# A list scheduler's rule for GpSimd: two-input work only beside VectorE work that leaves the shared port alone

## The chip, the cores and the metric

The kernel runs on one core of a Trainium2 chip. Five engines with queues of their own work on it: TensorE (PE in the profile) multiplies matrices into PSUM, VectorE (DVE), ScalarE (ACT) and GpSimd (POOL) work element by element, and SyncE (SP) issues the DMAs. The metric is device time of one execution in microseconds; the kernel before takes 1488.42 us, the median of three runs (1487.71 to 1492.01).

## The reference

Two layers run on 512 latent tokens (`x`) and 256 context tokens (`ctx`), 1024 channels each. In each layer an adaptive scale and shift, computed from `c`, gives `h`; one wide projection `h @ w_in` feeds three branches; the branches are gated, projected, mixed by sigmoid gates and projected out, and a layer norm closes the residual:

```python
h = x * (1.0 + scale[:, None, :]) + shift[:, None, :]
(a_q, a_k, a_v, a_g, g_q, g_k, g_v, g_af, g_ab, g_g,
 s_u, s_v, s_g, m_a, m_g, m_s) = jnp.split(h @ p['w_in'], pts, axis=-1)
...
y_attn = blocked_attention(ql, k_all, v_all) * jax.nn.silu(a_g)
...
y_gla = gla_finish(ol_f + flip(ol_b), p['gla_o_norm'], x.dtype) * jax.nn.silu(g_g)
y_sgu = sgu(s_u, s_v, p['sgu_ln_g'], p['sgu_ln_b'], p['sgu_w'], p['sgu_b']) * jax.nn.silu(s_g)
...
def merge(ya, yg, ys, ga, gg, gs):
    m = (jax.nn.sigmoid(ga) * (ya @ p['w_br_attn'])
         + jax.nn.sigmoid(gg) * (yg @ p['w_br_gla'])
         + jax.nn.sigmoid(gs) * (ys @ p['w_br_sgu']))
    return m @ p['w_out']

out = merge(y_attn, y_gla, y_sgu, m_a, m_g, m_s)
x_new = layer_norm(DEEPNORM_ALPHA * x + gate[:, None, :] * out, p['post_g'], p['post_b'])
```

The attention branch is grouped-query attention with normalised, rotated queries and keys over 768 keys. The second branch is bidirectional gated linear attention. The third, the gating MLP (`sgu`), normalises `s_v`, mixes positions inside chunks of 128 by a matrix and multiplies by `s_u`. Layer 1 computes outputs for the latent tokens alone.

## The kernel before

All matmuls run in a 32-bit format of TensorE with each operand split into a high and a low part: `split` lets ScalarE round a tile to `hi`, and an operation with two inputs subtracts, `lo = raw - hi`; `mm3` then issues three matmuls (high by high, high by low, low by high). So every 256 KB piece of a weight that a DMA brings (`raw`) costs one ScalarE copy and one subtraction, and the same holds for the activations (`hlh`, `hll` for the latent tokens' high and low parts, `hch`, `hcl` for the context's; `mlh`, `mll` for the merged branches). Weight pieces have three `raw` buffers and five each of `hi` and `lo`; the PSUM tags `p`, `pt` and `s` have two buffers each.

The stages of a layer, by the labels in the code: the modulation and the projections of attention (`P1`), the projections of the linear attention (`gproj`), projections whose results are kept in DRAM for later (`fill`), attention (`att`), the decays (`decay`), linear attention (`gla`, tiles `M`, `Ac`, `Af`), the gating of the branches (`ag`, `gg`; `kept` is a gate that is read back, `yat` and `oT` the branch outputs), the gating MLP (`sgu`: `sv` is normalised and multiplied by the two rows of `sgc`, mixed on TensorE into `pt`, evacuated into `ymix`, then multiplied by `kept` and by `sg`), the three branch projections (`brA`, `brG`, `brS`; `sig` and `sgS` are the gates, `mac` the sum) and the output projection (`out`; `rA` and `rB` hold the residual). The `sgc` rows take the buffer of `yat`, and so are loaded when `yat` has been split into `yh` and `yl`. In layer 1 the gate of the output is multiplied into the weight (`raw<-raw,gate`).

The program is not issued in the order of the code. Each operation is recorded by class `Sched` with its inputs, outputs and an assumed cost, and `order` then plays the whole program through: at each step it takes the engine that is free first and the ready operation of the smallest priority number, and so fixes each engine's queue. `issue` repeats this; after each pass the priorities move a share `MIX` of the way from the old start times to the latest starts that the pass allowed, and the pass with the shortest assumed length is issued.

Many operations are recorded with two possible engines: `tta` (issued in line 128) may run an operation with two inputs on VectorE or on GpSimd, `evac` a copy out of PSUM on ScalarE or VectorE. Whichever engine comes to the operation first takes it, with one exception, a test for GpSimd, which the change edits. `_port` tells the scheduler which operations use the port that VectorE and GpSimd share: on GpSimd all that read SBUF, on VectorE those with two wide SBUF inputs and some copies; `held` is the time up to which an engine holds it.

In the profile, all operations that one engine was fixed for stand under the recorder's line 419 and all that had a choice under line 128, so rows are told apart by their tiles.

Of the kernel before, what the change touches and what calls it, by code (L numbers as in the profile page):

```python
# [27 lines left out]
class Sched:  # L28
# [109 lines left out]
    def order(self, prio):  # L138
# [3 lines left out]
        ops = self.ops  # L142
# [22 lines left out]
        free = dict.fromkeys(engs, 0.0)  # L165
        ready = {e: [] for e in engs}
# [5 lines left out]
        held = {"DVE": 0.0, "POOL": 0.0}  # L172
        other = {"DVE": "POOL", "POOL": "DVE"}
        seq, when = [], [0.0] * n
        gone = [None] * n
        why, byat, lastop, relby = [None] * n, [None] * n, {}, {}
        costs = [0.0] * n
        hold = [[] for _ in range(n)]
        put = ()
        ends = [0.0] * n  # L180

        def freed(x, e):
# [34 lines left out]
        while done < n:  # L217
            best = None
            for e in engs:
                L, R = later[e], ready[e]  # L220
                while L and (L[0][0] <= free[e] or gone[L[0][1]]):
                    a, i = heapq.heappop(L)
# [4 lines left out]
                t = free[e] if R else (L[0][0] if L else None)  # L227
# [7 lines left out]
            t, e = best  # L235
            R, L = ready[e], later[e]
            while L and L[0][0] <= t:
                a, i = heapq.heappop(L)
                if not gone[i]:
                    heapq.heappush(R, (prio[i], i))  # L240
            i = None
# [4 lines left out]
            if e == "ACT" and len(R) > 1:  # L246
                c = min(R, key=lambda x: x[0] + (self.SWITCH if ops[x[1]][5] not in (None, cur) else 0))
                R.remove(c)
                heapq.heapify(R)
                i = c[1]  # L250
            elif e == "PE" and len(R) > 1:
                while recent and recent[0][0] < t - self.TICK:
                    dense -= recent.popleft()[1]
                if dense < self.WARM and ops[R[0][1]][8] < 0.5:
                    c = min(R, key=lambda x: x[0] + (1e6 if ops[x[1]][8] < 0.5 else 0))
                    R.remove(c)
                    heapq.heapify(R)
                    i = c[1]
                else:
                    i = heapq.heappop(R)[1]  # L260
            elif e in held and R and held[other[e]] > t + 1.0:

                w = held[other[e]] - t
                c = min(R, key=lambda x: x[0] + (self.HOLD * w if e in self.port[x[1]] else 0.0))
                R.remove(c)
                heapq.heapify(R)
                i = c[1]
            else:
                i = heapq.heappop(R)[1]
            if gone[i]:  # L270
                continue
            if e == "POOL" and isinstance(ops[i][4], dict) and len(ops[i][4]) > 1 and i not in put:

                back = max(0.0, free["DVE"] - t) + sum(ops[j][4]["DVE"] if isinstance(ops[j][4], dict) else ops[j][4] for p_, j in ready["DVE"] if not gone[j] and p_ < prio[i])
                if back + ops[i][4]["DVE"] < self.LEAVE * ops[i][4]["POOL"]:
                    heapq.heappush(later["POOL"], (t + max(back, 100.0) + ops[i][4]["DVE"], i))
                    continue
            k = can(i)
# [86 lines left out]
        for i in reversed(seq):  # L365
            e = gone[i]
# [9 lines left out]
        return seq, late, when, gone, costs, why  # L376

    SWITCH = 100.0
    HOLD, LEAVE = 1.0, 1.0
    ROUNDS, MIX, ADJ = 12, 0.35, ("PE",)  # L380
    SAME = {"DVE": 127.0, "ACT": 148.0, "POOL": 96.0}
    AHEAD = 3000.0
    TICK, COLS, WARM = 10240 / 3, 3060.0, 5500.0
# [1208 lines left out]
```

## Time and profile before

| | |
|---|---|
| median of three runs | 1488.42 us |
| lowest, highest | 1487.71, 1492.01 us |
| the profiled execution | 1490.06 us, span 1488.3 us |
| mean granted clock of TensorE | 0.975 of full speed |
| TensorE, VectorE, ScalarE, GpSimd busy | 95%, 70%, 45%, 29% of the span |

The span runs from the first to the last instruction; about 1.8 us of the profiled execution lie around it. A busy share is a mean over stages that are limited by different things, so what counts is which wait ends last in a stage. TensorE's clock has two levels, 2.4 and 1.2 GHz; the granted share of a stretch is 1.00 or 0.50 for these, or lies between where a stretch holds both. A duration of VectorE or GpSimd contains the time in which the instruction stood in the engine and waited for a port.

### The profile page before, as it was taken

Reading aid. Unit: us, or ns where it says so; the run is one execution under the profiler, and the core shown is the slowest. Engines: PE = TensorE matmul, PEld = TensorE weight load, DVE = VectorE, ACT = ScalarE, POOL = GpSimd, SP = SyncE. Lnnn points to the kernel's source line nnn. Section 1 sums busy time; section 2 is a strip of 40 time slices with the busy share of each in tenths; the row PEclk is TensorE's granted clock in tenths of the full one; section 3 lists DMA queues with packets and bytes.
Section 4 is the critical chain, followed back from the end, with each engine's and each line's share of the span. In section 5 each row is a group of like instructions: output and inputs, shape, how many; then the busy total and the mean of one; then the engine's idle time right before and its main releaser. Section 6 shows DMA issues by size and latency. Waiting matters only on the chain.

```text
span 1488.3 us, 27349 instructions
## 1 busy us (share of the span) xinstructions
PE 1409.4 (95%) x10724; PEld 1246.0 (84%) x10724; DVE 1039.7 (70%) x1996; ACT 672.9 (45%) x1286; POOL 435.9 (29%) x472
## 2 busy tenths in 40 slices
PE   8899999999986999999999999999999949999977
PEld 5798899888875888888889999988988738888877
DVE  8968887896878777432166675888797875443496
ACT  4466666844461223222231365667845632422321
POOL 1443230465864000100000043320367650000164
PEclk9999999999997999999999999999999969999989
DMA  9410012332272654321233232012343355334342
GB/s 327 142 37 9 22 30 77 105 91 93 69 244 65 191 158 139 91 68 54 68 104 102 100 91 63 16 29 77 116 136 93 88 183 156 102 94 102 98 142 93
DMA packets 115891, 151.23 MB, mean 102 GB/s; under 512 B 8601, under 2 KB 89905, under 8 KB 115761
## 3 DMA queue, kind: packets, MB, share of 16 engines
q1 hardware_dynamic: 115762, 149.49, 33.0%
q8 instruction: 84, 1.38, 0.4%
q14 instruction: 45, 0.37, 0.1%
HBM read 134.76 MB, written 14.69 MB: 100 GB/s over the span
## 4 chain that ended last, share of the span: by engine, by line
PE 79%; DVE 8%; ACT 4%; POOL 3%; DMA 3%; issue 2%; SPq 0%; POOLq 0%; ACTq 0%; DVEq 0%
PE p L419 64%; PE pt L419 9%; PE s L419 5%; PE s L119 2%; DVE sm L419 1%; ACT L419 1%; DVE lo L128 1%; DMA wada<-in_w_adaT_dram 1%; ACT ez L419 1%; DVE junk L419 1%; POOL ymix L128 1%; DVE wada L419 1%; DMA raw<-in_w_in_dram 1%; DVE PTs L419 1%; DMA sgc<-in_sgu_ln_g_dram 1%
## 5 line engine op out<-in xcount | busy, mean ns | idle before, releaser
L128 DVE TENSOR_TENSOR lo<-raw,hi 128x512 fp32r<-128x512 f32 (+1 forms) x265 | 202.8, 771 | 227.4 <-ACT hi L419 218.8
L419 ACT ACTIVATE hi<-raw 128x512 fp32r<-128x512 f32 (+1 forms) x296 | 186.2, 634 | 235.4 <-PE p L419 155.9
L419 PE MATMUL p<-hlh,hi 128*128 128x512 f32 x704 | 281.8, 401 | 8.6 <-ACT sg L419 6.6
L419 PE MATMUL p<-hlh,lo 128*128 128x512 f32 x704 | 281.0, 400 | 1.4 <-POOL lo L128 1.1
L419 PE MATMUL p<-hll,hi 128*128 128x512 f32 x704 | 280.1, 399 | 0.0
L419 PEld LDWEIGHTS p<-hlh,hi 128*128 128x128 f32 x704 | 133.1, 189 | 36.4 <-ACT sg L419 6.8
L419 PEld LDWEIGHTS p<-hlh,lo 128*128 128x128 f32 x704 | 133.2, 189 | 31.3 <-POOL lo L128 1.3
L419 PEld LDWEIGHTS p<-hll,hi 128*128 128x128 f32 x704 | 133.0, 189 | 26.9
L419 PE MATMUL p<-hch,hi 128*128 128x256 f32 x368 | 105.3, 286 | 8.9 <-ACT sg L419 7.9
L419 PE MATMUL p<-hch,lo 128*128 128x256 f32 x368 | 105.4, 287 | 0.0
L419 PE MATMUL p<-hcl,hi 128*128 128x256 f32 x368 | 105.0, 285 | 0.0
L419 PE MATMUL p<-lo,hlh 128*128 128x256 f32 (+1 forms) x352 | 101.0, 287 | 1.1 <-DVE lo L128 1.1
L419 PE MATMUL p<-hi,hlh 128*128 128x256 f32 (+1 forms) x352 | 101.3, 288 | 0.7 <-ACT keep L128 0.7
L419 PE MATMUL p<-hi,hll 128*128 128x256 f32 (+1 forms) x352 | 100.2, 285 | 0.0
L128 POOL TENSOR_TENSOR M<-cs 128x192 f32<-128x192 f32 (+1 forms) x144 | 82.0, 598 | 17.7 <-DVE cs L419 5.7
L419 ACT ACTIVATE sig<-p 128x512 f32<-128x512 f32 (+1 forms) x48 | 25.2, 526 | 131.3 <-PE p L419 131.0
L419 PEld LDWEIGHTS p<-hch,hi 128*128 128x128 f32 x368 | 70.6, 192 | 11.3 <-ACT sg L419 8.1
L128 POOL TENSOR_TENSOR raw<-raw,gate 128x512 f32<-128x512 f32 x10 | 16.8, 1682 | 201.0 <-DMA raw<-in_w_out_dram 200.9
L419 ACT ACTIVATE P<-s,sm 128x768 f32<-128x768 f32 (+1 forms) x80 | 65.3, 820 | 19.5 <-DVE sm L419 19.2
L419 DVE SCALAR_TENSOR_TENSOR wada<-wada,srow 128x512 f32<-128x512 f32 x96 | 69.7, 734 | 5.4 <-DMA wada<-in_w_adaT_dram 4.0
L419 PEld LDWEIGHTS p<-hcl,hi 128*128 128x128 f32 x368 | 70.4, 191 | 2.0
L419 DVE TENSOR_TENSOR PTs<-pt,PTs 128x512 fp32r<-128x512 f32 x104 | 69.5, 685 | 3.5 <-ACT PTs L419 1.9
(320 smaller groups left out, 3665.3 us busy)
## 6 DMA issues: line engine op xcount, KB each, us to landing
raw<-in_w_in_dram SPq DMA_DIRECT2D x204, 256.0 KB, 2.9
wada<-in_w_adaT_dram SPq DMA_DIRECT2D x80, 256.0 KB, 4.9
raw<-in_w_out_dram SPq DMA_DIRECT2D x32, 256.0 KB, 3.0
raw<-in_w_in_dram SPq DMA_DIRECT2D x16, 272.0 KB, 2.9
wada<-in_w_adaT_dram SPq DMA_DIRECT2D x8, 512.0 KB, 6.2
raw<-in_w_br_attn_dram SPq DMA_DIRECT2D x16, 256.0 KB, 3.3
raw<-in_w_br_gla_dram SPq DMA_DIRECT2D x16, 256.0 KB, 3.2
raw<-in_w_br_sgu_dram SPq DMA_DIRECT2D x16, 256.0 KB, 2.9
```

The costliest lines, as they stand in the source:

```text
L119: return self.record(eng.n, lambda: [getattr(eng.e, m)(*a, **k) for m, a, k in calls], outs, ins, cost, None, dens)
L128: fns[p.n] = lambda real=real, k=k: real(**k)
L419: return s.record(n, lambda: real(*a, **k), outs, ins, _cost(n, meth, outs, ins, k), _table(n, k), _dens(n, ins, k), _port(n, meth, outs, ...
```

## The change

The test for GpSimd reads differently. Before, GpSimd left a two-engine operation to VectorE if VectorE, with the rest of its current operation, its ready operations of smaller priority number and this one, would be done sooner than GpSimd alone. After, only that part of VectorE's pending work counts which does not use the shared port: GpSimd leaves the operation if that part is shorter than 0.8 of what GpSimd would take, and looks at it again later. Besides, the scheduler makes 16 passes where it made 12, and moves priorities by 0.6 of the way where it moved them by 0.35. Nothing that is computed changes; the line numbers of the recorder grow by 2 (L419 becomes L421).

```diff
-        put = ()
...
-            if e == "POOL" and isinstance(ops[i][4], dict) and len(ops[i][4]) > 1 and i not in put:
-
-                back = max(0.0, free["DVE"] - t) + sum(ops[j][4]["DVE"] if isinstance(ops[j][4], dict) else ops[j][4] for p_, j in ready["DVE"] if not gone[j] and p_ < prio[i])
-                if back + ops[i][4]["DVE"] < self.LEAVE * ops[i][4]["POOL"]:
+            if e == "POOL" and isinstance(ops[i][4], dict) and len(ops[i][4]) > 1:
+
+                dve = lambda j: ops[j][4]["DVE"] if isinstance(ops[j][4], dict) else ops[j][4]
+                mine = [(dve(j), "DVE" in self.port[j]) for p_, j in ready["DVE"] if not gone[j] and j != i and p_ < prio[i]]
+                apart = max(0.0, free["DVE"] - max(t, held["DVE"])) + sum(c for c, p_ in mine if not p_)
+                back = max(0.0, free["DVE"] - t) + sum(c for c, _ in mine)
+                if apart < self.LEAVE * ops[i][4]["POOL"]:
                     heapq.heappush(later["POOL"], (t + max(back, 100.0) + ops[i][4]["DVE"], i))
                     continue
...
-    HOLD, LEAVE = 1.0, 1.0
-    ROUNDS, MIX, ADJ = 12, 0.35, ("PE",)
+    HOLD, LEAVE = 1.0, 0.8
+    ROUNDS, MIX, ADJ = 16, 0.6, ("PE",)
```

The order of the instructions on each engine shows what this moves. GpSimd's queue has 477 instructions before and 228 after, VectorE's 1822 and 2078.

GpSimd in the last stage of layer 1, where the weights of the output projection (`raw`) are multiplied by the gate and the merged branches get their low parts (`mll`); before:

```order
L128 TENSOR_TENSOR ymix<-ymix,sg 128x512
L128 TENSOR_TENSOR raw<-raw,gate 128x512 x2
L128 TENSOR_TENSOR mll<-mac_2149,mlh 128x512
L128 TENSOR_TENSOR raw<-raw,gate 128x512
L128 TENSOR_TENSOR mll<-mac_2150,mlh 128x512
L128 TENSOR_TENSOR raw<-raw,gate 128x512
L128 TENSOR_TENSOR lo<-raw,hi 128x512
```

GpSimd after, from the last copies of layer 1's linear attention on:

```order
L421 COPY Af<-Ac 32x4x32 x4
L421 TENSOR_SCALAR sg<-sg 128x4
L421 TENSOR_TENSOR sg<-sg,mhalf 128x4
L421 TENSOR_SCALAR sf<-sf 128x1
L421 TENSOR_TENSOR sf<-sf,mhalf 128x1
L421 TENSOR_TENSOR rA<-rA,pg 128x416 x2
```

All of the gating MLP, the branches and the output weights has left this queue; what remains is fixed to GpSimd.

VectorE in layer 1's gating MLP; before:

```order
L128 TENSOR_TENSOR sv<-sv,sgc 128x512 x5
L419 TENSOR_TENSOR ymix<-pt,sgc 128x4x128
L419 SCALAR_TENSOR_TENSOR wada,gs<-wada,srow 128x512
L419 TENSOR_TENSOR ymix<-pt,sgc 128x4x128
L419 SCALAR_TENSOR_TENSOR wada,gs<-wada,srow 128x512
L419 TENSOR_TENSOR ymix<-pt,sgc 128x4x128 x2
L128 TENSOR_TENSOR ymix<-ymix,kept 128x512 x2
L128 TENSOR_TENSOR ymix<-ymix,sg 128x512 x3
```

VectorE there after (`wada` is a product for the adaptive gate that is summed on the way):

```order
L128 TENSOR_TENSOR sv<-sv,sgc 128x512 x7
L421 TENSOR_TENSOR ymix<-pt,sgc 128x4x128
L128 TENSOR_TENSOR sv<-sv,sgc 128x512
L421 TENSOR_TENSOR ymix<-pt,sgc 128x4x128
L421 SCALAR_TENSOR_TENSOR wada,gs<-wada,srow 128x512
L421 TENSOR_TENSOR ymix<-pt,sgc 128x4x128
L421 SCALAR_TENSOR_TENSOR wada,gs<-wada,srow 128x512
L421 TENSOR_TENSOR ymix<-pt,sgc 128x4x128
L128 TENSOR_TENSOR ymix<-ymix,kept 128x512 x2
L128 TENSOR_TENSOR ymix<-ymix,sg 128x512 x2
```

All eight products of `sv` stand in this queue now, where three were on GpSimd, and the first two `sg` products follow two `kept` products at once.

TensorE just ahead of the same stage; before:

```order
L419 MATMUL p<-hll,hi 128x512
L419 MATMUL p<-hlh,lo 128x512
L419 MATMUL pt<-ident,o 128x128 x4
L419 MATMUL pt<-sgc,sv 128x128 x16
L419 MATMUL p<-hlh,hi 128x512
```

TensorE there after:

```order
L421 MATMUL p<-hlh,hi 128x512
L421 MATMUL p<-hll,hi 128x512
L421 MATMUL p<-hlh,lo 128x512
L421 MATMUL pt<-sgc,sv 128x128 x16
L421 MATMUL p<-hlh,hi 128x512
```

The mixing matmuls (`pt<-sgc,sv`) stood right behind the last transposes of the linear attention (`pt<-ident,o`); now projections stand between them. Between the last `s<-M` matmul of the linear attention and the first mixing matmul there are 18 matmuls of 512 columns before and 69 after in layer 1; in layer 0 there are 58 of 512 and 51 of 256 before, 71 and 67 after, and 24 of 256 and 2 of 512 after stand between the mixing matmuls.

## Rows read from the trace of the kernel before

**Rows 1.** The page's first part: busy time, share of the span and number of instructions of an engine.

```profile
span 1488.3 us, 27349 instructions
PE 1409.4 (95%) x10724; PEld 1246.0 (84%) x10724; DVE 1039.7 (70%) x1996; ACT 672.9 (45%) x1286; POOL 435.9 (29%) x472
```

**Rows 2.** The waits of TensorE over the whole span: who waited for whom, us in total, how often, the longest in us.

```profile
PE p L419 <- ACT sg L419: 14.5, 2, 7.9
PE pt L419 <- DVE sv L128: 13.5, 1, 13.5
PE s L419 <- ACT hlh L419: 8.5, 5, 2.4
PE pt L419 <- POOL sv L128: 8.4, 1, 8.4
PE p L419 <- DVE rA L419: 3.6, 2, 3.3
...
PE p L419 <- POOL mll L128: 1.9, 1, 1.9
...
PE p L419 <- ACT mlh L419: 1.4, 2, 0.7
...
PE p L419 <- DVE sgS L419: 0.8, 1, 0.8
```

**Rows 3.** Busy time by stretch, around the two gating MLPs: the stretch, its length, then busy us (and instructions) of PE, PEld, DVE, ACT and POOL, the granted clock of TensorE, the DMA share and GB/s.

```profile
452.00:458.00 6.00, 6.00 (x28) 6.00 (x29) 3.47 (x6) 0.00 (x0) 4.51 (x3) 0.50 0.00 0
...
469.20:475.20 6.00, 5.91 (x26) 5.81 (x27) 4.12 (x9) 1.02 (x3) 1.30 (x1) 0.50 0.03 12
...
1210.40:1216.00 5.60, 5.56 (x26) 5.57 (x27) 4.77 (x9) 0.00 (x0) 1.11 (x1) 0.51 0.24 80
...
1223.40:1229.50 6.10, 6.04 (x14) 4.78 (x15) 3.49 (x9) 3.15 (x5) 0.00 (x0) 0.50 0.18 37
```

**Rows 4.** Groups of VectorE's instructions from 1225 to 1400 us, a stretch in which GpSimd does nothing: line, engine, operation, tiles, shapes, count, then busy us, mean ns of one, idle us before them and what ended it.

```profile
L128 DVE TENSOR_TENSOR lo<-raw,hi 128x512 fp32r<-128x512 f32 x63 | 43.5, 691 | 89.0 <-ACT hi L419 88.9
...
L419 DVE TENSOR_TENSOR sig<-p,sig 128x512 f32<-128x512 f32 x8 | 5.5, 692 | 4.8 <-PE p L419 4.8
```

**Rows 5.** The same groups of VectorE from 1405 to 1441 us, the last stage, in which GpSimd works too (`sgS` reads `p` in PSUM).

```profile
L128 DVE TENSOR_TENSOR mac<-mac,sgS 128x512 f32<-128x512 f32 x7 | 10.2, 1464 | 0.0
L128 DVE TENSOR_TENSOR lo<-raw,hi 128x512 fp32r<-128x512 f32 x6 | 6.3, 1052 | 0.0
L419 DVE TENSOR_TENSOR sgS<-p,sgS 128x512 f32<-128x512 f32 x7 | 4.8, 680 | 0.6 <-PE p L419 0.6
```

**Rows 6.** GpSimd's largest group in the same stretch.

```profile
L128 POOL TENSOR_TENSOR raw<-raw,gate 128x512 f32<-128x512 f32 x8 | 14.1, 1769 | 186.3 <-DMA raw<-in_w_out_dram 186.2
```

**Rows 7.** VectorE's timeline at 1187 us: start, length of the merged piece in us, engine, line, operation, tiles, shapes, count.

```profile
1187.62 1.28 DVE L128 TENSOR_TENSOR lo<-raw,hi 128x512 fp32r<-128x512 f32 x2
```

**Rows 8.** The chain of work that ended last, pieces in order of time (start us, us, what), in the gating MLPs of layer 0 and layer 1.

```profile
442.45 4.30 DMA sgc<-in_sgu_ln_g_dram
...
450.23 1.71 POOL sv L128
...
451.99 5.50 PE pt L419 x24
...
462.77 6.06 POOL ymix L128 x3
...
1202.69 3.64 DMA sgc<-in_sgu_ln_g_dram
...
1208.64 1.76 DVE sv L128
...
1210.44 6.45 PE pt L419 x32
...
1217.68 5.11 POOL ymix L128 x3
...
1223.46 2.93 PE p L419 x6
```

**Rows 9.** Busy time by stretch as in rows 3, in the start, in layer 1's attention, in its linear attention and in its branch projections.

```profile
37.00:74.00 37.00, 32.59 (x167) 27.43 (x166) 36.61 (x97) 17.07 (x33) 17.18 (x13) 0.91 0.47 143
...
910.00:1050.00 140.00, 136.78 (x984) 126.31 (x983) 116.41 (x220) 92.23 (x197) 34.11 (x31) 1.00 0.14 39
...
1080.00:1120.00 40.00, 40.00 (x403) 32.49 (x402) 37.92 (x89) 19.76 (x41) 26.86 (x48) 1.00 0.45 126
...
1225.00:1355.00 130.00, 130.00 (x555) 105.18 (x554) 59.88 (x105) 43.10 (x73) 0.00 (x0) 0.98 0.40 112
```

**Rows 10.** Busy time by stretch of the instructions of line 128 alone, those that had a choice of engine: the stretch, its length, busy us (and instructions) of DVE, ACT and POOL, the granted clock, the DMA share and GB/s.

```profile
910.00:1050.00 140.00, 41.49 (x59) 3.15 (x7) 26.41 (x20) 1.00 0.14 39
...
1080.00:1195.00 115.00, 60.86 (x91) 6.74 (x12) 60.42 (x90) 1.00 0.40 115
...
1405.00:1445.00 40.00, 33.14 (x23) 0.00 (x0) 27.14 (x15) 0.87 0.40 132
```

**Rows 11.** The longest wait of VectorE over the whole span, columns as in rows 2.

```profile
DVE lo L128 <- ACT hi L419: 218.8, 87, 13.8
```

## The prediction

> **What bounds the kernel now.** I read the page's first part first. TensorE is busy 95% of a span of 1488.3 us, VectorE 70%, GpSimd 29% [rows 1]. So the most that a new division of work between VectorE and GpSimd can return is the time that TensorE stands still, and what its clock loses behind that. The waits of TensorE come next [rows 2]: the shown groups are 52.6 us, and four single waits make up most of it. 13.5 us and 8.4 us are for the first normalised tile of the gating MLP (`sv`), one in each layer, and 14.5 us in two waits (7.9, and 6.6 by difference) for ScalarE's `sg`, which itself waits for a buffer that a `ymix` product frees. Another 7.7 us are in the last projection (3.6 for `rA`, 1.9 for `mll` on GpSimd, 1.4 and 0.8). The start has 8.5 us.
>
> The two mixing stages show a second cost behind the waits, TensorE's clock [rows 3]: after the idle time it runs at its lower level of 1.2 GHz (granted 0.50 or 0.51) for 6.0 and 5.9 us of work in layer 0, 5.6 and 6.0 us in layer 1. Half of that is lost: 3 us each.
>
> Why the stages wait is read from durations. In a stretch where GpSimd has nothing to do a 128x512 subtraction of two SBUF tiles takes VectorE 691 ns, and one that reads PSUM 692 ns [rows 4]. In the last stage, beside GpSimd, the product `mac` takes 1464 ns and `lo` 1052 ns, while `sgS`, which reads PSUM, takes 680 ns [rows 5]. GpSimd needs 1769 ns for a product of that size there [rows 6]. Two VectorE subtractions back to back end in 1.28 us, so one costs its queue 0.64 us [rows 7].
>
> Here the Trainium skill, SBUF — State Buffer, Who interferes with whom, has a rule: a VectorE instruction with two SBUF inputs and a GpSimd instruction that reads SBUF exclude each other, and the later one blocks until the other ends. The trace agrees on who suffers (`mac`, not `sgS`) but not fully on how much: by a full block the 27.14 us of GpSimd in the last stage would all be lost to VectorE, while its 23 products there took 33.14 us [rows 10] for about 19.2 (by the order 16 of 0.64 and 7 of twice the width at 1.28), 13.9 lost. By the rule the last stage would give its whole 7.7 us of waits back; I go by the row, below.
>
> **The change part by part.** The new test leaves GpSimd a two-input operation only if VectorE has work without the port for at least 0.8 of its time. By the order, 248 of GpSimd's 327 such operations go to VectorE (30 of 31 `lo`, 84 of 144 `M<-cs`, all 10 `raw` products, 7 of 9 `sv`). All engines' queues are reordered by the new iteration; TensorE's instructions and the DMAs are the same set.
>
> *Layer 1's mixing.* Now the first `sv` products run from 1206.3, when `sgc` has landed, to 1210.4, and the `ymix` products on GpSimd take 5.11 us [rows 8]. TensorE restarts its large matmuls at 1223.46. After the change all eight `sv` are on VectorE: the first pair takes 2 x 0.64 = 1.3 us instead of 4.0. And the order puts 69 matmuls of 512 columns between the end of the linear attention and this point, 18 before. At 130 us for 555 [rows 9] one is 0.234 us, so 51 more are 11.9 us of cover. 11.9 + 2.7 is over 13.5: the first wait goes. Behind it the order has 15 VectorE operations up to the first `sg` product (6 `sv`, 4 `ymix<-pt`, 2 of the modulation, 2 `kept`, 1 `sg`), 9.6 us, where 12.4 pass now (1210.4 to 1222.8, the end of `ymix`): 2.8 saved. What is late next there is this VectorE queue alone, so some 4 us of the second wait stay, and its clock loss; the first clock loss (2.8) goes. Sum 13.5 + 2.8 + 2.8 = 19.1 us.
>
> *Layer 0's mixing.* The same way [rows 8]: `sgc` lands at 446.75 and TensorE starts at 451.99, 5.2 us that become 1.3 (3.9 saved). The cover is 13 matmuls of 512 and 16 of 256 columns more, 3.0 + 1.9 = 4.9 us. Together 8.8: the wait of 8.4 goes. Inside the stage the order now has 24 matmuls of 256 columns, 2.8 us, which weren't there. The VectorE queue to the first `sg` product is 18 x 0.64 + 2 x 0.96 (768 wide), 13.4 us, and one tile's two products stay on GpSimd, 2.6 us at twice VectorE's price: 16.0 against 16.9 (451.9 to 468.8). So 0.9 + 2.8 = 3.7 of the second wait, and 3.0 of clock. Sum 15.1 us.
>
> *The last stage.* 38 two-SBUF operations are now spread over 33.14 us of VectorE and 27.14 us of GpSimd in 40 us [rows 10]. All on VectorE they cost 30 x 0.64 + 8 x 1.28 = 29.4 us, and the PSUM reads among them (7 `sgS` at 0.68, some `rA` and statistics) about 7: 36.4, so 3.6 us less. Bounds 0 and the 7.7 of the waits; I take 4.
>
> *The start* (8.5 us of waits for `hlh` [rows 2]): VectorE is full there, 36.61 of 37 us [rows 9]. The 13 operations that keep GpSimd busy 17.18 us in that stretch come on top of it, at some 0.64 each 8 us, and the time that they take from VectorE by contention goes. I take +2, bounds -3 and +6.
>
> *What it costs.* The 51 and 13 matmuls were cover inside the linear attention. There the order has 66 fewer of 512 columns in layer 1 (15.4 us) and 33 of 512 with 16 of 256 fewer in layer 0 (9.6 us). Unless that stage becomes shorter by as much, TensorE waits in it instead. Its bound is the pair of engines: in 1080:1195 two-input work keeps VectorE busy 60.86 and GpSimd 60.42 us, together 121 in 115 [rows 10]. GpSimd's 90 operations there become 32. The 58 cost 58 x 0.67 = 38.9 us on GpSimd; on VectorE 42 small ones of 128 columns (an estimate: 0.3, half of what a four times wider one costs) and 16 at 0.64 are 22.8. That frees 16 us in layer 1, about the 15.4 that it must. Both ends: 0 and 25.0. Since a stage is not its busiest engine alone, I take 12, between the row and the worst end. Attention has VectorE at 116.41 of 140 us [rows 9] with 20 two-input operations on GpSimd, of which most move; their own contention goes with them too. Bounds -2 and +10, taken 3.
>
> Sum: 19.1 + 15.1 + 4 + 2 - 12 - 3 = 25 us off the profiled execution's 1490.06 (span 1488.3 and 1.8 around it): 1465. The runs' median, 1488.42, is 1.6 lower, so the forecast is 1463.5.
>
> **The rivals.** *The cover was only moved.* The linear attention does not get shorter, and the mixing is held by what VectorE never set (the `sgc` transfer of 3.64 and 4.30 us, ScalarE's `yh`). Then 25 us of new waits stand against half of the 34.2 and the 6 of the other two terms: 1490.1 - 23.1 + 25 = 1492, 1490.4 at the median. For it speaks that TensorE is already busy nearly everywhere and the total of its work is the same. Against it speak the two full port engines [rows 10].
>
> *VectorE becomes the bound.* Its queue is in order, and 248 operations more stand in it. Now `lo` waits for ScalarE's `hi` 87 times, 218.8 us, 2.5 each [rows 11]; while it waited, GpSimd took others. The 30 moved `lo` alone bring 75 us of such waits, and behind each stand the PSUM evacuations that free TensorE's banks. It decides where VectorE's row is full already, 37.92 of 40 us in 1080:1120 and 36.61 of 37 in 37:74 [rows 9]. If a quarter of the 75 falls there, 19 us, and the linear attention costs its full 25, the sum is 40.2 - 25 - 19 - 3 = -7: 1495 at the median, slower. Against it: contention there takes about as much of VectorE as the moved work needs. The Trainium skill, Perfetto Trace Analysis, Optimizing Scalar/DVE Operations, speaks for this rival: it says that with VectorE saturated handing work to GpSimd may make sense, though it adds that the shared port may undo it. By that rule the full rows above forbid the move; the trace's 1464 ns [rows 5] against 691 [rows 4] sides with its second half.
>
> *Nothing new waits.* Both costs are 0, the last stage gives 7.7 and the start 6: 19.1 + 15.1 + 7.7 + 6 = 48 us, 1440.5. Against it: so full a recovery needs each queue's new order to fit the chip's times.
>
> That the change does not do what it says is excluded by the order's counts.
>
> **How the numbers follow.** Forecast 0.62, cover only moved 0.12, VectorE the bound 0.10, nothing new waits 0.16. A measurement of this kernel can tell about 0.3%, 4.5 us, from no change. Forecast and last rival are faster, with a quarter of the first rival: 0.81. Of the first rival 0.07 more and of the second 0.02 are the same, 0.09; the rest, 0.10, is slower. The forecast's own range, with costs from 30 down to 2, is 1478 to 1450; to hold 8 of 10 beside the rivals on both sides it becomes 1447 to 1487.
>
> **What would show it.** Right: GpSimd's busy time falls from 436 us to about 140, VectorE's stays near 1040 (its products at 0.69 us again); the waits of 13.5 and 8.4 for `sv` are gone or under 2 us; GpSimd's name is gone from the chain in the mixing stages; `mac` in the last stage is under 0.8 us. Wrong: the waits of TensorE add up to 50 us or more as now, with new entries in the linear attention (`M`, `Ac`, `Af`), or in attention for `PTs` and `sm`, or VectorE's busy time rises above 1100 us.

## The result and the profile after

The changed kernel takes 1451.32 us (median of 4 runs, 1449.73 to 1453.14), the kernel before beside it 1488.74 us (4 runs). The ratio is 0.9745 with a 95% interval of 0.9724 to 0.9767: 37.4 us faster. The forecast was 1463.5 us, so the direction was right, the time lies inside the range, and the gain was half as large again as the 25 us forecast.

The first part of the page, after; it answers to [rows 1]:

```profile
span 1448.0 us, 27281 instructions
PE 1397.2 (96%) x10724; PEld 1232.3 (85%) x10724; DVE 1041.7 (72%) x2252; ACT 664.4 (46%) x1275; POOL 140.8 (10%) x223
```

GpSimd has lost two thirds of its work, and VectorE's busy time has grown by only 2.0 us although 248 operations came to it, since those that it already had became shorter: its 254 `lo` of 128x512 were busy for 192.3 us at 762 ns each, the 279 after for 191.6 at 693. The span is 40.3 us shorter. It splits into two parts: span less busy time of TensorE falls from 78.9 to 50.8 us, 28.1 us less standstill; and the same 10,724 matmuls are busy for 12.2 us less, at a higher granted clock (mean 0.994, before 0.975).

The waits of TensorE, after, in the columns of [rows 2]:

```profile
PE pt L421 <- DVE sv L128: 5.1, 2, 4.2
PE s L119 <- DVE M L128: 5.0, 5, 1.7
PE p L421 <- ACT sg L421: 3.9, 1, 3.9
PE s L119 <- DVE Ac L421: 3.0, 4, 1.3
...
PE s L421 <- ACT hlh L421: 2.3, 1, 2.3
```

The waits for `sv` fall from 21.9 us to 5.1 (0.9 in layer 0, 4.2 in layer 1), those for `sg` from 14.5 to 3.9. `Ac` is new and `M` has grown from 1.6 us to 5.0, both in the linear attention. All waits of TensorE add up to 41.0 us, before to 70.3.

Where the time went is read from stretches bounded by the same instructions in both kernels. Busy time by stretch, in the columns of [rows 3], before: the start up to the first scores; layer 0's linear attention (first to last matmul of `M`); layer 0's mixing (from there to 200 matmuls behind the last `pt<-sgc,sv`); layer 1's linear attention; layer 1's mixing (to 100 matmuls behind); the last stage (from its first output matmul to 300 before the end).

```profile
0.00:99.26 99.26, 88.45 (x474) 73.86 (x474) 82.57 (x220) 47.38 (x92) 29.61 (x33) 0.95 0.53 179
307.54:418.96 111.42, 110.08 (x1913) 95.71 (x1913) 92.89 (x168) 51.57 (x91) 78.41 (x105) 1.00 0.26 77
418.96:505.94 86.98, 68.95 (x402) 61.24 (x393) 64.83 (x107) 30.16 (x49) 34.64 (x24) 0.88 0.54 178
1092.16:1188.83 96.67, 96.08 (x1304) 76.69 (x1303) 83.00 (x174) 54.66 (x97) 66.41 (x104) 1.00 0.36 102
1188.83:1249.24 60.41, 39.23 (x201) 32.56 (x179) 40.77 (x65) 20.59 (x33) 19.00 (x13) 0.77 0.58 189
1421.68:1444.13 22.45, 15.41 (x85) 14.08 (x86) 22.28 (x19) 2.53 (x4) 17.11 (x9) 0.78 0.34 123
```

The same six stretches, after:

```profile
0.00:93.55 93.55, 84.14 (x468) 69.00 (x468) 76.26 (x233) 47.55 (x94) 6.24 (x16) 1.00 0.55 189
297.43:404.44 107.01, 101.92 (x1865) 88.06 (x1864) 97.45 (x216) 48.67 (x86) 38.37 (x58) 1.00 0.27 82
404.44:477.83 73.39, 72.44 (x457) 63.77 (x446) 55.73 (x109) 31.33 (x51) 4.49 (x4) 1.00 0.62 191
1069.52:1160.80 91.28, 82.49 (x1238) 65.53 (x1237) 82.03 (x211) 44.31 (x83) 27.34 (x51) 0.98 0.31 88
1160.80:1217.89 57.09, 49.05 (x251) 40.15 (x229) 39.91 (x76) 22.81 (x39) 1.20 (x2) 0.94 0.68 214
1389.49:1402.63 13.14, 10.72 (x86) 10.12 (x85) 13.14 (x18) 2.21 (x4) 0.00 (x0) 0.99 0.44 151
```

Since matmuls have moved between the stretches, a stretch is credited with what it now holds more and charged with what it holds less, each at the spacing that its kind had before. Layer 0's mixing is 13.6 us shorter and holds 9.6 us more: a gain of 23.2. The part of a gain that is standstill is the change of length less PE's busy time. The rest is the time that the matmuls themselves took more or less; where the granted clock rose with it, it is put down to the clock.

| stretch | forecast | gain | of it standstill | rest |
|---|---|---|---|---|
| start | 2 | 5.0 | 10.8 to 9.4: 1.4 | 3.6 |
| linear attention, layers 0 and 1 | -12 | -5.1, -9.9 | 1.3 to 5.1, 0.6 to 8.8: -12.0 | -3.0 |
| layer 0's mixing | 15.1 | 23.2 | 18.0 to 1.0: 17.1 | 6.1 |
| layer 1's mixing | 19.1 | 15.2 | 21.2 to 8.0: 13.1 | 2.1 |
| last stage | 4 | 9.3 | 7.0 to 2.4: 4.6 | 4.7 |
| attention, both | -3 | 0.4 | | |

The rows add up to 38.1 us of the 40.3 by which the span is shorter; the other 2.2 lie between these stretches.

Groups of VectorE in the last stage, after (1368 to 1401 us); they answer to [rows 5]:

```profile
L128 DVE TENSOR_TENSOR lo<-raw,hi 128x512 fp32r<-128x512 f32 x9 | 6.2, 686 | 1.8 <-ACT hi L421 1.8
...
L421 DVE TENSOR_TENSOR sgS<-p,sgS 128x512 f32<-128x512 f32 x8 | 5.5, 685 | 1.5 <-PE p L421 1.5
L128 DVE TENSOR_TENSOR mac<-mac,sgS 128x512 f32<-128x512 f32 x8 | 5.5, 684 | 0.0
```

`mac` has gone from 1464 ns to 684, `lo` from 1052 to 686, and `sgS`, which reads PSUM, has stayed (680, 685).

### The profile page after: what moved, and what is told of

It is laid out like the page before. It is cut to its first block, busy times and chain, and to the rows that moved or that the text cites. A ratio compares the mean times of both kernels' runs of the same rounds, so it can differ in the third digit from the quotient of the medians.

```text
span 1448.0 us, 27281 instructions
## 1 busy us (share of the span) xinstructions
PE 1397.2 (96%) x10724; PEld 1232.3 (85%) x10724; DVE 1041.7 (72%) x2252; ACT 664.4 (46%) x1275; POOL 140.8 (10%) x223
## 5 line engine op out<-in xcount | busy, mean ns | idle before, releaser
L421 PE MATMUL p<-hlh,hi 128*128 128x512 f32 x704 | 281.6, 400 | 6.1 <-ACT sg L421 3.9
L421 ACT ACTIVATE hi<-raw 128x512 fp32r<-128x512 f32 (+1 forms) x296 | 185.2, 633 | 220.0 <-PE p L421 145.4
L421 PE MATMUL p<-hll,hi 128*128 128x512 f32 x704 | 280.8, 399 | 0.0
L421 PE MATMUL p<-hlh,lo 128*128 128x512 f32 x704 | 280.5, 399 | 0.0
L421 PEld LDWEIGHTS p<-hlh,hi 128*128 128x128 f32 x704 | 132.7, 188 | 34.0 <-ACT sg L421 4.1
L421 PEld LDWEIGHTS p<-hlh,lo 128*128 128x128 f32 x704 | 132.9, 189 | 30.1 <-DVE lo L128 1.1
L421 PEld LDWEIGHTS p<-hll,hi 128*128 128x128 f32 x704 | 132.6, 188 | 26.2
L421 PE MATMUL p<-hch,lo 128*128 128x256 f32 x368 | 104.3, 283 | 0.0
L421 PE MATMUL p<-hcl,hi 128*128 128x256 f32 x368 | 104.3, 283 | 0.0
L421 PE MATMUL p<-hch,hi 128*128 128x256 f32 x368 | 104.2, 283 | 0.0
L421 PE MATMUL p<-hi,hlh 128*128 128x256 f32 (+1 forms) x352 | 101.7, 289 | 0.0
L421 PE MATMUL p<-hi,hll 128*128 128x256 f32 (+1 forms) x352 | 100.5, 286 | 0.0
L421 PE MATMUL p<-lo,hlh 128*128 128x256 f32 (+1 forms) x352 | 99.9, 284 | 0.0
L421 ACT ACTIVATE sig<-p 128x512 f32<-128x512 f32 (+1 forms) x48 | 25.3, 527 | 129.7 <-PE p L421 128.8
L421 POOL TENSOR_SCALAR sf<-sf 128x1 f32<-128x1 f32 x20 | 10.1, 505 | 687.5 <-DVE sf L421 687.0
L421 ACT ACTIVATE P<-s,sm 128x768 f32<-128x768 f32 (+1 forms) x80 | 65.3, 820 | 23.5 <-DVE sm L421 22.9
L421 DVE TENSOR_REDUCE sm<-s 128x1 f32<-128x768 f32 (+1 forms) x72 | 64.8, 921 | 9.6 <-PE s L421 9.5
L421 DVE TENSOR_TENSOR PTs<-pt,PTs 128x512 fp32r<-128x512 f32 x104 | 69.5, 684 | 2.7 <-ACT PTs L421 2.0
L421 PEld LDWEIGHTS p<-hch,hi 128*128 128x128 f32 x368 | 69.5, 189 | 2.0
L421 DVE SCALAR_TENSOR_TENSOR wada<-wada,srow 128x512 f32<-128x512 f32 x96 | 65.5, 689 | 7.7 <-DMA wada<-in_w_adaT_dram 6.3
L421 PEld LDWEIGHTS p<-hcl,hi 128*128 128x128 f32 x368 | 69.3, 188 | 2.1
```

Of the source, the lines that this page charges most:

```text
L421: return s.record(n, lambda: real(*a, **k), outs, ins, _cost(n, meth, outs, ins, k), _table(n, k), _dens(n, ins, k), _port(n, meth, outs, ...
```

## The experiments

Two causes had to be told apart: the freed port (which engine runs an operation) and the new order of all queues; and two parts of the change, the test and the larger steps. A third possible cause, that VectorE is simply the faster engine for such an operation (0.64 us for a product [rows 7], where GpSimd's shortest of that size takes 1.28), stands beside the port in the first pair of runs and is taken up at the added loads. "Kept" is the number of two-engine operations that GpSimd keeps; the kernel before has 327, the changed kernel 79. Matmuls and length of the linear attention are for layer 0 and layer 1, between the ends used above; each ratio is to the kernel before, run beside it.

| kernel | kept | us | ratio, 95% interval | linear attention, us | matmuls in it |
|---|---|---|---|---|---|
| before | 327 | 1488.7 | | 111.4, 96.7 | 1912, 1302 |
| changed | 79 | 1451.3 | 0.9724 to 0.9767 | 107.0, 91.3 | 1863, 1236 |
| old order, new engines | 79 | 1483.4 | 0.9945 to 0.9974 | 115.1, 98.2 | 1912, 1302 |
| new order, old engines | 327 | 1498.7 | 1.0048 to 1.0078 | 111.9, 88.8 | 1863, 1236 |
| test alone | 86 | 1446.1 | 0.969 to 0.9722 | 104.4, 93.0 | 1863, 1251 |
| steps alone | 325 | 1488.5 | 0.9989 to 1.0008 | 109.0, 97.6 | 1907, 1306 |
| none kept, large steps | 0 | 1475.3 | 0.9887 to 0.9923 | 116.7, 101.3 | 1936, 1295 |
| none kept, small steps | 0 | 1472.7 | 0.9873 to 0.9909 | 117.5, 98.6 | 1935, 1295 |
| test outside linear attention | 193 | 1462.7 | 0.9808 to 0.9839 | 111.1, 96.8 | 1917, 1288 |
| test in linear attention only | 223 | 1483.3 | 0.9947 to 0.9975 | 113.5, 96.2 | 1898, 1286 |
| share 0.5 | 111 | 1448.6 | 0.9703 to 0.9762 | 106.1, 89.1 | 1845, 1247 |
| share 1.2 | 41 | 1464.6 | 0.9817 to 0.9852 | 112.8, 95.4 | 1873, 1267 |

**Order and engines, one at a time.** The scheduler plans under both tests; the order of one plan is issued, and operations that may run on GpSimd take the engine of the other plan:

```diff
+        mine, other = self.plan(False), self.plan(True)
...
-            (fn[self.gone[i]] if isinstance(fn, dict) else fn)()
+            e = self.gone[i]
+            if isinstance(fn, dict) and "POOL" in fn:
+                e = other[3][i]
+            (fn[e] if isinstance(fn, dict) else fn)()
```

> The sequence of the kernel before, instruction by instruction, but every two-engine operation with GpSimd as a choice goes to the engine that the kernel after gives it (79 instead of 327 on GpSimd). Port theory (the gain comes from operations that no longer shut each other out): much of the 37 us is there without any new order, 1460 to 1475 us; mac in the last stage near 0.7 us, the last stage 5 us or more shorter. Order theory (the gain comes from the new sequence, which keeps projections as cover for the gating MLP): 1483 us or more, since the wait for sv in layer 1 stays over 8 us with 18 matmuls of cover.

Measured: 1483.4 us. The waits of TensorE:

```profile
PE pt L430 <- DVE sv L128: 19.2, 2, 11.8
PE p L430 <- ACT sg L430: 10.8, 2, 6.2
```

This is what the order theory named: with the engines alone the two large waits stay, because TensorE has nothing to do until `sgc` has landed and `sv` is made. The port theory was nearly right on the last stage alone: `mac` takes 684 ns, and the stage is 4.7 us shorter. By stretches the engines alone gain 14.5 us in the start, the mixing and the last stage, and lose 13.9 in attention and the linear attention, under an order that was not planned for them.

The reverse, with `plan(True)` as `mine`:

> The sequence of the kernel after, but each two-engine operation on the engine that the kernel before gave it (327 on GpSimd). Port theory: the gain is lost, 1480 us or more, and since that sequence was laid out for other engines it may be slower than the kernel before (1490 to 1510). Order theory: most of the gain stays, 1452 to 1465 us.

Measured: 1498.7 us, slower than before, as the port theory named. The waits:

```profile
PE s L430 <- ACT kt L430: 9.1, 3, 4.2
PE s L119 <- DVE M L128: 8.4, 10, 2.2
PE pt L430 <- DVE sv L128: 7.4, 1, 7.4
...
PE pt L430 <- POOL sv L128: 5.4, 1, 5.4
```

The waits for `sv` shrink even with GpSimd at its old work, since the matmuls kept back cover them: the mixing stages gain 15.0 and 7.9 us, reckoned as above, where engines alone gave 3.7 and 4.2 and the change 23.2 and 15.2. But the stages that lent the matmuls pay: `kt` and `M` are waited for, the decays and linear attention lose 6.0 + 10.0 us in layer 0, 8.2 + 7.4 in layer 1. So most of the mixing's gain is the order's, and the new division of work is what makes that order affordable. Engines alone give 6 us, order alone -10, together 37: neither of the two theories holds by itself. Since neither mixed kernel runs an order planned for its engines, the two numbers are no prices of port and order, and they do not tell the freed port from VectorE's shorter time for an operation.

**Test and steps, one at a time.** With the new test and the old 12 passes and 0.35:

```diff
-    ROUNDS, MIX, ADJ = 16, 0.6, ("PE",)
+    ROUNDS, MIX, ADJ = 12, 0.35, ("PE",)
```

> The new test with its factor 0.8, but 12 passes and steps of 0.35 as before (86 two-input operations on GpSimd). If the rule makes the gain: 1450 to 1460 us. If the larger steps make it: 1475 us or more.

And with the old test and the new steps:

```diff
...
-                if apart < self.LEAVE * ops[i][4]["POOL"]:
+                if back + ops[i][4]["DVE"] < self.LEAVE * ops[i][4]["POOL"]:
...
-    HOLD, LEAVE = 1.0, 0.8
+    HOLD, LEAVE = 1.0, 1.0
```

> 16 passes and steps of 0.6, the test of the kernel before (325 two-input operations on GpSimd). If the rule makes the gain: 1480 to 1492 us. If the larger steps make it: under 1465 us.

Measured: 1446.1 and 1488.5 us. The test does it all; the larger steps do nothing by themselves and cost some 5 us on top of the test (the two intervals, 0.969 to 0.9722 and 0.9724 to 0.9767, do not meet). The test alone has the lowest median of the study. The largest part of its lead, 4.3 us, lies in the linear attention (losses of 2.5 and 8.2 us instead of 5.1 and 9.9); layer 1's mixing and the last stage give 1.9 us each back.

**What GpSimd keeps.** 60 of the 79 kept operations are `M<-cs`. Taking all 79 away:

```diff
-    HOLD, LEAVE = 1.0, 0.8
+    HOLD, LEAVE = 1.0, 1000000000.0
```

> The changed kernel with the test's share set so high that GpSimd gets none of the 79 two-input operations with a choice that it keeps; 16 passes and 0.6 stay. Theory (beside PSUM work GpSimd's product costs VectorE nothing, so the kept operations are a gain): VectorE has some 79 x 0.4 = 30 us more to do, most of it where it idles, and the time is 0 to 8 us longer than the changed kernel, 1451 to 1459. Rival (every read of GpSimd disturbs VectorE, the rule has only made most of them disappear): 5 us or more shorter, 1446 or less.

The same with small steps:

> The same with 12 passes and a share of 0.35, so it stands to the run of the rule alone (1446.1) as the run before it stands to the changed kernel. Theory: 1446 to 1454, and the difference to the run with large steps is again some -5 us if small steps are better in themselves. Rival (the 5 us between the rule alone and the changed kernel are the luck of one order): the two runs without any choice lie the other way round or within 2 us.

Measured: 1475.3 and 1472.7 us. Theory had the sign, not the size: the kept operations are worth 24 and 27 us, three times the upper bound. Busy time by stretch, none kept and large steps: linear attention and mixing of layer 0, then of layer 1.

```profile
307.20:423.90 116.70, 114.44 (x1937) 99.41 (x1937) 103.68 (x240) 54.69 (x94) 17.41 (x30) 0.99 0.27 82
423.90:502.13 78.23, 61.05 (x359) 54.21 (x351) 63.97 (x137) 26.98 (x45) 2.67 (x2) 0.87 0.56 186
1089.58:1190.84 101.26, 95.89 (x1296) 75.13 (x1296) 88.26 (x244) 54.56 (x95) 15.63 (x28) 1.00 0.34 95
1190.84:1245.20 54.36, 37.85 (x192) 31.41 (x169) 35.86 (x69) 20.25 (x33) 1.20 (x2) 0.78 0.59 186
```

With VectorE alone on `M`, the linear attention is 9.7 and 10.0 us longer than in the changed kernel and runs 73 and 59 matmuls more; the mixing then has fewer (359 and 192 recorded, against 457 and 251) and stands still for 17.2 and 16.5 us, near the old 18.0 and 21.2. Reckoned as above, the two mixing stages gain 1.7 and 3.9 us where they gained 23.2 and 15.2, and the linear attention loses 6.2 us less: together some 27 us, the difference of the spans. That the longer linear attention uses the matmuls up is a reading and is shown only in part. VectorE is busy there for 6.2 us more in each layer (103.7 and 88.3 against 97.5 and 82.0), but the added matmuls are themselves 12.0 and 13.8 us of work, and no run takes the 79 away under the changed kernel's order. Small steps are 2.6 us better here too, but these two intervals overlap, so that small steps are better in general stays open.

**Where the test acts.** The new test with the old one for operations labelled linear attention, and the reverse (`not gla`), both with small steps:

```diff
-                if apart < self.LEAVE * ops[i][4]["POOL"]:
+                old = back + ops[i][4]["DVE"] < ops[i][4]["POOL"]
+                gla = (ops[i][7] or "").endswith("gla")
+                if (old if gla else apart < self.LEAVE * ops[i][4]["POOL"]):
```

> The rule alone (12 passes, 0.35), with the old test for the operations labelled linear attention: GpSimd gets 193 operations with a choice instead of 86. Theory 1 (the gain lies in the gating MLP, the branches and the last stage, where GpSimd's products stood in front of TensorE's restarts): 1446 to 1458, nearly the whole gain, since the order may still put cover there. Theory 2 (VectorE freed of contention in the linear attention is what lets matmuls be kept back as cover): 1468 to 1480, and the waits for sv return to 8 us or more.

> The reverse: the new test for the operations labelled linear attention alone, the old test elsewhere, 12 passes and 0.35; GpSimd gets 223. Theory 1: 1478 to 1489, with GpSimd's sv, ymix and raw products in the chain as before. Theory 2: 1455 to 1470, the waits for sv under 3 us although GpSimd still has such products.

Measured: 1462.7 us, between the two theories, and 1483.3 us, as theory 1 has it. The first has the start and the last stage of the test alone (5.6 and 7.3 us gained), but waits 17.2 us for `sv`, as theory 2 said:

```profile
PE pt L423 <- DVE sv L128: 17.2, 2, 10.4
```

25.8 and 5.2 us of gain make 31, where the test in both places made 43.0: the other 12 us need the new test in both places. That cover is made in one stage and used in the next would explain it; these two runs do not show it by themselves.

**The port by itself.** In the changed kernel GpSimd is all but idle while layer 1 mixes (1.2 us of 57.1). In each layer 16 products are put into the mixing that read `sgc` and write a tile that nobody reads:

```diff
+                for _ in range(16):
+                    nc.gpsimd.tensor_tensor(out=spare, in0=lg_[:, 0:256], in1=lg_[:, 256:512], op=ALU.mult)
```

> The changed kernel with 16 products of 128x256 added on GpSimd in each layer's gating MLP, which read the loaded sgc and write a spare tile that nobody reads; they start when sgc has landed and take some 15 us a layer by the 0.93 us of a product of that size. In layer 0 they stand ahead of GpSimd's own two sv products, which come up to 15 us later. Port theory: VectorE's products beside them stretch, by about half of GpSimd's time as in the last stage of the kernel before (13.9 of 27.14 us), 7 us a layer, and the time grows by 10 to 25 us over 1451, by at least 6 us more than in the control with memsets. Rival (contention costs little, the order did it all): within 3 us of the control.

In the control:

```diff
+                nc.gpsimd.tensor_tensor(out=spare[:, 0:1], in0=lg_[:, 0:1], in1=lg_[:, 0:1], op=ALU.mult)
+                for _ in range(48):
+                    nc.gpsimd.memset(spare, 0.0)
```

> The control: one product of one column, then 48 memsets of 128x256 at the same place on GpSimd (some 10 to 15 us a layer), so its queue is as long but reads nothing wide. Port theory: VectorE's products keep their 0.6 to 0.7 us, layer 1 costs nothing, layer 0 only what its two late sv products cost: 1451 to 1459. Rival: as much longer as with the reads.

Measured: 1471.7 us (ratio 0.9863 to 0.9899) and 1466.1 us (0.9826 to 0.9865). Timelines of GpSimd and VectorE in layer 1, with the reads (start us, us):

```profile
1196.97 17.69 POOL L1529 TENSOR_TENSOR spare<-sgc 128x256 f32<-128x256 f32 x16 [13.65 <-DMA sgc<-in_sgu_ln_g_dram]
```

```profile
1196.92 1.82 DVE L128 TENSOR_TENSOR sv<-sv,sgc 128x512 f32<-128x512 f32 x2 [1.73 <-DMA sgc<-in_sgu_ln_g_dram]
1198.91 5.50 DVE L128 TENSOR_TENSOR sv<-sv,sgc 128x512 f32<-128x512 f32 x5 [0.16 <-DMA sgc<-in_sgu_ln_b_dram]
1204.33 0.68 DVE L421 TENSOR_TENSOR ymix<-pt,sgc 128x512 f32<-128x512 f32 x1
...
1209.61 2.20 DVE L128 TENSOR_TENSOR ymix<-ymix,kept 128x512 f32<-128x512 f32 x2
1211.73 2.34 DVE L128 TENSOR_TENSOR ymix<-ymix,sg 128x512 f32<-128x512 f32 x2
...
1215.74 1.28 DVE L128 TENSOR_TENSOR ymix<-ymix,sg 128x512 f32<-128x512 f32 x2
```

With the memsets:

```profile
1198.26 17.70 POOL L1530 MEMSET spare<- 128x256 f32 x48
```

```profile
1197.46 4.30 DVE L128 TENSOR_TENSOR sv<-sv,sgc 128x512 f32<-128x512 f32 x7 [1.32 <-DMA sgc<-in_sgu_ln_g_dram]
1201.68 0.68 DVE L421 TENSOR_TENSOR ymix<-pt,sgc 128x512 f32<-128x512 f32 x1
...
1206.02 1.29 DVE L128 TENSOR_TENSOR ymix<-ymix,kept 128x512 f32<-128x512 f32 x2
1207.23 1.29 DVE L128 TENSOR_TENSOR ymix<-ymix,sg 128x512 f32<-128x512 f32 x2
...
1209.64 1.29 DVE L128 TENSOR_TENSOR ymix<-ymix,sg 128x512 f32<-128x512 f32 x2
```

GpSimd is busy equally long in both. Beside its reads five `sv` take 5.50 us, beside its memsets seven take 4.30; `ymix<-pt,sgc`, with one input in PSUM, takes 0.68 in both. From the first `sv` to the end of the fourth `sg` product VectorE needs 20.1 us (1196.92 to 1217.02) beside reads and 13.5 (1197.46 to 1210.93) beside memsets: 6.6 us lost to 17.69 us of reads, some 0.6 of them idle. This is the contention of [rows 5], made on purpose, with the same engine for every operation of the kernel in both runs. Layer 1's mixing takes 62.7 us against 54.4, 8.3 more: 3.9 of standstill, and 4.5 of longer matmuls at a granted clock of 0.86 against 0.97. Over the whole kernel it is 5.6 us, a little under the 6 named; layer 0 goes the other way by 1.1. The control's stage is itself 2.7 us shorter than the 57.1 of the changed kernel (`sgc` lands 1.2 us sooner in it), so against the changed kernel the reads cost that stage 5.6. The pair prices the port in one stage; how the whole gain divides between the port and VectorE's shorter time for an operation stays open.

The control's time missed its expectation: 1466.1 against 1451 to 1459. In layer 0 GpSimd's two `sv` products come behind the memsets, and TensorE waits 13.6 us for the later one; I had priced that at 8 at most.

The Trainium skill, SBUF — State Buffer, Who interferes with whom, calls the shared port an exclusive lock between such instructions. The pair of runs agrees on which instructions suffer. That VectorE lost 37% of GpSimd's 17.69 us, and not all, does not speak against a lock, since GpSimd's time holds waits of its own: of its products the shortest take 0.72 us, the median 1.05. Where the two engines alternate, one `sv` and one GpSimd product take 1.13 us together (the spacing of the stretched `sv`); undisturbed their spacings are 0.60 and 0.80, so a full exclusion would be 1.40 by this estimate. The prediction's figure for the last stage, 13.9 lost of 27.14, has the same flaw: GpSimd's `raw` products there take 1769 ns, the shortest in that kernel 1280.

**The share.** The test alone with another share in the place of 0.8:

> The rule alone (12 passes, 0.35) with a share of 0.5 in place of 0.8: GpSimd keeps 111 operations with a choice (86 at 0.8, none in the run without). If what GpSimd keeps in the linear attention shortens that stage and lets matmuls be held back for the mixing, a few more there cost or gain little: 1442 to 1452, LA and mixing gains within 3 us a stage of the rule alone. Rival (few is best, each read disturbs): 1452 to 1465.

> The same with a share of 1.2: GpSimd keeps 41. First theory: fewer kept means a longer linear attention that uses up the matmuls itself, so the time lies between the rule alone (1446) and the run with none (1472.7), 1452 to 1466, with sv waits of 5 to 17 us. Rival: within 3 us of the rule alone.

Measured: 1448.6 us, not to be told from the changed kernel or the test alone, and 1464.6 us, both inside the range of the first theory. The stages of the first did not stay within the 3 us named: against the test alone layer 0's linear attention costs 4.4 us more and layer 1's mixing gains 4.9 more. With 0, 41, 86 and 111 kept the time is 1472.7, 1464.6, 1446.1 and 1448.6 us: here some work must stay on GpSimd. The linear attention shortens from 117.5 to 112.8, 104.4 and 106.1 us in layer 0, from 98.6 to 95.4, 93.0 and 89.1 in layer 1, but it also holds fewer matmuls (see the table), so its length alone does not tell which caused which.

## Why the prediction was right, and which terms were mis-sized

**The mechanism** was as put, in the main. Matmuls leave the linear attention and cover the mixing: the 51 of layer 1 that were priced at 11.9 us are in its stretch (121 matmuls instead of 70 up to the last `pt<-sgc,sv`, 11.9 us of work). The linear attention pays with standstill, 12.0 us by the stretches. That this equals the number taken is luck: 12 was picked between 0 and 25.0. That the order needs the new division of work, and the division the order, is shown by the two mixed kernels; that reads of GpSimd cost VectorE time, by the two added loads. The terms missed in both directions (from -3.9 to +8.1 us) and left the forecast 12.2 us too long.

**The clock was left out of three terms.** This is the larger part of the miss. The forecast gave back lost clock only where the half-clock windows of [rows 3] had been read, 5.8 us. The *last stage* has gained 9.3 us against 4. Its standstill gave 4.6, near the term; the other 4.7 is the clock: the same 84 matmuls are busy for 10.7 us at 0.99 where it was 15.4 at 0.78. The *start* gave 1.4 us of standstill, against 2, and 3.6 of clock (0.95 to 1.00). Both clocks could be seen before: [rows 9] has 0.91 in 37:74, [rows 10] 0.87 in the last stage. In *layer 0's mixing* only one clock loss of 3.0 was given back, and both went (6.1).

**Layer 0's mixing, 15.1 forecast, 23.2 measured.** The step that was mis-sized, beside the clock, is "16.0 against 16.9". VectorE's timeline after:

```profile
431.69 4.37 DVE L128 TENSOR_TENSOR sv<-sv,sgc 128x512 f32<-128x512 f32 x7 [3.70 <-DMA sgc<-in_sgu_ln_g_dram]
...
443.97 1.82 DVE L128 TENSOR_TENSOR ymix<-ymix,kept 128x768 f32<-128x768 f32 x2
445.71 1.96 DVE L128 TENSOR_TENSOR ymix<-ymix,sg 128x512 f32<-128x512 f32 x4
```

The sum charged GpSimd's two products, 2.6 us, to VectorE's queue, and took the queue's end as that of the wait. The queue reaches the first `sg` product 14.0 us after it started (431.69 to 445.71), and the two `sv` on GpSimd delay nothing in it. With 9.6 us more of matmuls in the stage TensorE has no second wait left at all: 8.6 us went (7.9 for `sg` and 0.7 for `ymix`) where 3.7 had been taken.

**Layer 1's mixing, 19.1 forecast, 15.2 measured.** "The first wait goes" failed: 4.2 us of 13.5 stay. The second wait came out as put, 3.9 left of 6.6; 1.1 us that the sum did not count went too, and the clock gave back 2.1 for 2.8. The chain of waits after, from the last matmuls of `M` on, and behind it the line of the chain before that answers to the first:

```profile
1160.63 0.39 PE s L119 x32
1161.01 1.82 PE p L421 x7
...
1164.67 5.33 PE p L421 x23
1169.99 0.64 PE pt L421 x4
...
1176.36 5.50 DMA sgc<-in_sgu_ln_g_dram
1181.88 1.12 DVE sv L128 x2
...
1183.83 3.68 PE pt L421 x16
```

```profile
1188.66 0.39 PE s L119 x32
```

The cover is there, but what it must cover ends later. `sgc` is issued 15.7 us after the last matmuls of `M` (1160.63) where it was 14.0 (1188.66 to 1202.69), and takes 5.50 us instead of 3.64 [rows 8]: it lands 3.6 us later. The forecast held that time fixed. The chain also shows 30 matmuls of `p` (7 and 23) ahead of the branch's transposes (`pt` x4), where 18 stood before; so 12 of the 51 that were meant as cover stand in front of what releases `sgc`. Why the transfer takes longer stays open. The clock is between its two levels over two stretches there, so at 1.2 GHz for part of each:

```profile
1184.00:1190.00 6.00, 5.44 (x32) 5.18 (x32) 5.85 (x13) 0.00 (x0) 0.00 (x0) 0.72 0.36 138
...
1193.30:1200.00 6.70, 6.68 (x22) 5.32 (x23) 4.97 (x11) 3.70 (x5) 0.00 (x0) 0.75 0.32 91
```

**Linear attention and attention.** -15.0 against -12: behind the 12.0 of standstill 3 us of longer matmuls were not counted. Their cause stays open; the granted clock there is 1.00 and 0.98. Attention, priced at -3, did not change.

**The rivals.** *VectorE becomes the bound* needed longer waits for `hi`; after:

```profile
DVE lo L128 <- ACT hi L421: 206.5, 78, 13.4
```

It was 218.8 us before [rows 11]. The Trainium skill, Perfetto Trace Analysis, Optimizing Scalar/DVE Operations, warns that offloading between VectorE and GpSimd might not help. By the runs it depends on what is offloaded: taking 248 operations from GpSimd, in an order planned for it, gained 37 us, and taking the other 79 too cost 24. *Cover only moved* is what the kernel with the new order and the old engines shows: 1498.7 us; with the new engines the mixing's gain of 38.4 us is over twice the linear attention's loss. That the two full port engines decide it, as argued, is not shown apart from VectorE's shorter times. *Nothing new waits* fell on the linear attention's 15 us; its terms for the last stage and the start, 7.7 and 6, were nearer to the 9.3 and 5.0 measured than the forecast's.

Of the signs named, GpSimd's 140.8 us, VectorE's 1041.7 and `mac` at 684 ns came, and GpSimd is gone from the chain in layer 1's mixing (layer 0's is not on the chain after). The `sv` wait of layer 1 is over the 2 us named. Of the signs against, `M` and `Ac` came, but all waits together are 41.0 us, not 50.

## What to carry to other kernels

Two engines that share a port should split work by what each operation reads, and the choice should be known to whatever lays out the order: here the new assignment under the old order gave 6 us, the new order under the old assignment cost 10, and both gave 37. When a wait is expected to go, look up the granted clock of the same stretch, since here 12.2 of the 40.3 us by which the span fell came as shorter busy time of the same matmuls. Cover is lent by another stage: ask what shortens that stage, and whether the covering work stands ahead of what it should wait for.

## What the runs showed of the hardware that was not expected

Which of GpSimd's operations disturb VectorE was expected in the control; how clearly it shows was not. GpSimd's memsets of 128x256 leave VectorE's products at 684 ns (median of 18 `sv`) in the same time in which its reads bring them to 1209 ns, although both kinds write SBUF. And a small share of GpSimd, 31.3 us of `M<-cs` in the whole span, together with 19 other operations, was worth 24 us of device time where 0 to 8 had been expected; by the reading above, it decided how many matmuls another stage had left.
